# A hybrid RWKV-7 / latent-attention layer: TensorE's order in the recurrence stage written out by hand

## The chip, the cores and the metric

The kernel runs on one core of a Trainium2 chip. The metric is the device time of one execution in microseconds. Before the change three runs took 2447.49, 2455.89 and 2457.13 us, median 2455.89 us.

## What is computed

One layer over 2048 tokens of width 1024, in float32. One input projection feeds an RWKV-7 branch (8 heads of 64), a latent-attention branch (8 heads) and two sigmoid gates; the gated sum of the branches goes through an output projection, a norm and a residual add. Cut to what the change touches:

```
u    = rmsnorm(h, g_pre)
proj = u @ w_in                       # 1024 x 5152
feat_a, z_a, c_q, c_kv, k_pe, z_b, gate_logits = split_cols(proj, ...)

# RWKV-7 branch, per head, over the tokens t in order
f = feat + mu * (prev(feat) - feat);  r, k, v, wd, ad = split_cols(f, ...)
w = exp(-DECAY_SCALE * sigmoid(w0 + tanh(wd) @ w_decay_up));  a = sigmoid(a0 + ad @ w_iclr_up)
kk = k * k_k / max(norm(k * k_k), 1e-12);  k = k * (1 + (a - 1) * k_a)
sa = S @ -kk_t
S  = S * w_t + sa (kk_t * a_t)^T + v_t k_t^T
y_t = S @ r_t
y = groupnorm(y) + sum(r * k * r_k) * v
y_a = (y * silu(z_a)) @ w_out_a
# latent attention on c_q, c_kv, k_pe gives y_b (not touched)
merged = sigmoid(g_a) * y_a + sigmoid(g_b) * y_b
h = h + rmsnorm(merged @ w_o, g_post)
```

## The kernel before

**Stages.** The sequence is four segments of 512 tokens (NS) for the projection and eight half-steps of 256 tokens (NH) for the recurrence, each of four chunks of 64 tokens. The program writes: the projection of segment 0 (`proj_seg(0)`), the element work of half-step 0 (`elem(0)`), then in turn recurrence steps and projections of segments 1 to 3, then steps 5 to 7, preparations for attention, step 8 and the gate columns (`gates_seg`). Attention and the output stage follow. From about 185 us to 1142 us the recurrence's small products run with projection matmuls between them.

**The projection.** `proj` (L287) and `mm3` (L279) compute one tile of 128 columns by 512 tokens, `pj`, in 24 matmuls: for each of eight row blocks three (L283 to L285), since weight and input are each split into a high and a low part (`whl`; `xh`, `xl`). `make_xT` (L207) normalises x and transposes it (`xps`). Weights come over SP's DMA queue (`load_w`, L253). A tile's result is shifted by a token and written to memory (`fsh`), or copied (`lat`). `gates_seg` (L487) does the same for 42 gate tiles; when a segment's X isn't the one in place, it reloads it (`load_xT`).

**The recurrence.** `step(k)` (L833) works on half-step k and finishes half-step k-1:

- `zblock` (L637) multiplies the half-step's vectors into the blocks `pz`, masked to `Zr` by DVE (L646), one per chunk; pieces go to memory (`d_q`).
- `gather` (L653) reads them back as `Xg`, and `invert` (L691) inverts small triangular blocks by 60 DVE operations in pairs (L698, L700), writes the result to `d_q` and reads it as `Xinv`. `merge` (L716) joins the blocks: DVE's `XT` (L721), PE's `pf` and `px` (L726, L735), copies into `Zr` (L743).
- `chunk` (L745) of half-step k-1 is a chain between engines: `ch` from `Zr` (L756), ACT's `rs`, `ch` from `Xinv` (L772), ACT's `uv`, `ch` from `BT` (L778), DVE's new `uv` (L782), which the next chunk needs. The `Y` products (L296, L301, L785) collect its output y.
- `gnorm` (L794) normalises y, transposes it (`ypt`, L814) and adds the bonus, which it reads from and writes to memory (`bvb`, `d_ya`, L818 to L820). `tokmaj` (L663) transposes `bs` and `vf` (`pb`, `pv`).
- `elem` (L509) prepares half-step k+1: norms (`n`, `Rn`), three `bc` tiles (L551, evacuated at L553), then for each of four head pairs the logits `wa` (L585), the normalisation `rn` (L604) and DVE, ACT and POOL work (`cum` L592, `kkn`, `AR`, `BK`, `bv`). `bc`, `wa`, `rn` and `bo` share one PSUM buffer.

**Order.** Engines work in order, each on its own list. Before the change a list scheduler with a simulated timeline orders all engines: it takes an instruction when its inputs are ready by its own costs, and by place in the program among those that are ready. A step runs `elem`, `invert`, `gnorm` and `tokmaj` as generators and takes them in turn by a string, in the program's order only:

```python
for ch in "itietiegtietietii":
    next({"i": inv, "t": tm, "g": gn, "e": el}[ch], None)
```

Of the kernel before, what the change touches and what calls it, by code (L numbers as in the profile page):

```python
# [49 lines left out]
def hybrid_layer(ctx, tc, x, positions, g_pre, w_in, b_gate, mu_shift, w0, w_decay_up, a0, w_iclr_up, k_k, k_a,  # L50
# [156 lines left out]
    def make_xT(pool, psp, ptag, pbufs, s, g_rep, Xs):  # L207

        XH, XL = Xs
        for i in range(4):  # L210
# [18 lines left out]
            for k in range(2):  # L229
# [63 lines left out]

    def pin(*args, **kw):

        tc.keep_in_program_order(PE.matmul(*args, **kw))  # L296
# [7 lines left out]
    with st:  # L304
# [19 lines left out]
        NZ = 6  # L324
# [106 lines left out]
        def proj_seg(s):  # L431
            make_xT(sa, ppa, "pj", 2, s, g_rep, X)
# [10 lines left out]
            proj(ps, wtile(1536, elo=G if s else V, keep=later(0)), X, 2)  # L443
# [3 lines left out]
            yield  # L447
            for p in range(NP):
                ps = pj()
                proj(ps, wtile(512 + p * P, keep=later(p)), X)  # L450
                f = shift(ps, 4 + p)
                nc.sync.dma_start(d_f["k", p, s], f)
                yield
            for i, c0 in enumerate((C_CQ, C_CQ + P, C_CKV)):
                ps = pj()
                proj(ps, wtile(c0, keep=later(i)), X)
# [3 lines left out]
                yield  # L460

            for p in range(NP):
                for nm, c0, j in (("r", 0, 0), ("v", 1024, 8)):
                    ps = pj()
                    proj(ps, wtile(c0 + p * P, keep=later(j // 8)), X)
                    f = shift(ps, j + p)
                    nc.sync.dma_start(d_f[nm, p, s], f)
                    yield
# [3 lines left out]
            proj(ps[0:HD, :], load_w(sa, None, KC, HD, pieces=[(0, 32, k1), (32, 16, k1[:, 16:32]),  # L472
# [12 lines left out]
            yield  # L485

        def gates_seg():  # L487

            xs = NS - 1
            for s, i in d_zg:  # L490
                if s != xs:
                    xs = s
                    load_xT(X, s)
                ps = pj()
                c0 = (C_ZA, C_ZB, C_G, C_G + 4 * P, C_G + 8 * P, C_G + 12 * P)[i // 4] + (i % 4) * P
                proj(ps, wtile(c0), X)
# [7 lines left out]
                yield  # L504
# [4 lines left out]
        def elem(hs, E):  # L509
# [11 lines left out]
            for p in range(NP):  # L521
# [6 lines left out]
                          skip_group_check=True)  # L528
            lats = []
            for i in range(3):  # L530
# [7 lines left out]
                          skip_group_check=True)  # L538
            nr = t_("sqe", 2)
# [8 lines left out]
            for i in range(3):  # L548
# [7 lines left out]
                G.dma_start((d_cq[s][:, i, :, :] if i < 2 else d_kv[s])[:, :, cs_], lhl)  # L556
            hl = [se.tile([P, 256], F32R, name=f"hl{k}", tag=f"hl{k}", bufs=1) for k in range(2)]
# [19 lines left out]
            for p in range(NP):  # L577
# [24 lines left out]
                G.tensor_scalar(ta, ta, 0.5, 0.5, op0=ALU.mult, op1=ALU.add)  # L602
                rn = pp.tile([P, 2, 256], F32, name="rn", tag="e", bufs=1)
# [23 lines left out]
                if p == NP - 1:  # L627
                    bo = pp.tile([P, 2, 256], F32, name="bo", tag="e", bufs=1)
                    bonus(bo[:, 1], *last)()
# [61 lines left out]
        def invert(hs, E):  # L691
# [3 lines left out]
            for s_ in range(1, 31):  # L695
# [5 lines left out]
                if s_ % 5 == 0:  # L701
                    yield
# [11 lines left out]
            yield  # L714

        def merge(hs, E):  # L716
# [12 lines left out]
            for h in range(2):  # L729
                A.copy(FT[h * HD + 32:h * HD + 64], pf[h * HD + 32:h * HD + 64])  # L730
# [702 lines left out]
```

## Time and profile before

| | before |
|---|---|
| median of three runs | 2455.89 us |
| the profiled execution, and its span | 2453.57 us, 2451.8 us |
| PE busy in the span | 2211.4 us (90%) |
| DVE, ACT, POOL busy | 1089.6 (44%), 712.1 (29%), 1017.4 us (41%) |
| mean granted clock of PE | 0.950 |
| chain that ended last | PE 57%, DVE 16%, DMA 14% |
| merges (`pf`) of steps 0 to 7 begin at | 270, 405, 509, 619, 742, 864, 979, 1075 us |

The span is the time from the first to the last instruction. PE is TensorE, DVE VectorE, ACT ScalarE, POOL GpSimd, SP the engine that issues most DMAs. A busy PE is one with a matmul in it, at whatever clock; the granted clock is a share of 2.4 GHz, so 1.00 is that and 0.50 is 1.2 GHz, and values between are means over a stretch. Idle time before an instruction is put down to the instruction or DMA that ended it.

### The profile page before, as it was taken

The numbers are of one execution on the slowest core, as the hardware profiler recorded it, in microseconds if no ns is written. First come the engines' busy times: TensorE is split into PE (matmuls) and PEld (weight loads), VectorE is DVE, ScalarE is ACT, GpSimd is POOL, SyncE is SP. The second block draws the span as 40 slices with busy tenths as digits, with TensorE's granted clock in tenths as the row PEclk, the third lists the DMA queues.
The fourth block names the chain that finished last, engine by engine and source line by source line (L and its number), as shares of the span: only waits on it lengthen the run. The fifth ranks groups of instructions, "written<-read, shape, count | busy, mean of one in ns | idle before, by whom it ended". The sixth has DMA issues, their size and how long they took to land.

```text
span 2451.8 us, 37859 instructions
## 1 busy us (share of the span) xinstructions
PE 2211.4 (90%) x14313; PEld 1644.0 (67%) x14313; DVE 1089.6 (44%) x2007; ACT 712.1 (29%) x1283; POOL 1017.4 (41%) x1194
## 2 busy tenths in 40 slices
PE   6968989988979898997799998988999989999997
PEld 5747767767757676775555655555678867788876
DVE  7166575678374847434453534345130231300312
ACT  4343242343224343122233333332331211111111
POOL 6474352455254645222345653554533232312422
PEclk9969999989989999999798999999999999999999
DMA  7768867647658788673221112050396885766873
GB/s 249 229 190 276 258 194 232 172 125 220 187 169 247 208 254 262 181 216 104 65 82 31 50 58 76 28 190 7 106 367 224 290 309 197 287 203 202 317 243 120
DMA packets 315182, 455.15 MB, mean 186 GB/s; under 512 B 114044, under 2 KB 207288, under 8 KB 309368
## 3 DMA queue, kind: packets, MB, share of 16 engines
q1 hardware_dynamic: 285112, 406.06, 51.8%
q0 software_dynamic: 12608, 42.47, 5.3%
q10 hardware_dynamic: 17280, 4.20, 1.1%
q8 instruction: 113, 1.85, 0.3%
q14 instruction: 69, 0.57, 0.1%
HBM read 313.69 MB, written 132.64 MB: 182 GB/s over the span
## 4 chain that ended last, share of the span: by engine, by line
PE 57%; DVE 16%; DMA 14%; POOL 5%; issue 3%; ACT 2%; SPq 1%; ACTq 0%; DVEq 0%; POOLq 0%
PE pj L283 7%; PE pst L296 7%; PE pj L284 7%; PE pj L285 7%; PE po L296 5%; DVE mx L1055 3%; DMA wraw<-in_w_in_dram 2%; DMA whl<-d_wi 2%; PE pout L283 2%; PE pout L284 2%; PE pout L285 2%; PE py L283 2%; PE py L284 2%; PE py L285 2%; DVE Xg L700 2%
## 5 line engine op out<-in xcount | busy, mean ns | idle before, releaser
L283 PE MATMUL pj<-xh,whl 128*128 128x512 f32 (+1 forms) x1320 | 531.3, 403 | 31.3 <-DMA whl<-d_wi 13.9
L285 PE MATMUL pj<-xh,whl 128*128 128x512 f32 (+1 forms) x1320 | 526.4, 399 | 2.4 <-POOL whl L248 2.4
L284 PE MATMUL pj<-xl,whl 128*128 128x512 f32 (+1 forms) x1320 | 525.5, 398 | 0.0
L1178 POOL TENSOR_TENSOR acc<-acc,pt 128x1024 f32<-128x1024 f32 (+2 forms) x144 | 290.6, 2018 | 206.9 <-PE po L296 179.6
L283 PEld LDWEIGHTS pj<-xh,whl 128*128 128x128 f32 x1320 | 252.9, 192 | 97.8 <-issue 12.1
L285 PEld LDWEIGHTS pj<-xh,whl 128*128 128x128 f32 x1320 | 252.5, 191 | 63.0 <-POOL whl L248 4.2
L284 PEld LDWEIGHTS pj<-xl,whl 128*128 128x128 f32 x1320 | 253.0, 192 | 55.9 <-issue 2.5
L1055 DVE TENSOR_REDUCE mx<-pm 128x2 f32<-128x1024 f32 (+3 forms) x160 | 164.5, 1060 | 150.4 <-PE pm L296 149.7
L248 POOL TENSOR_TENSOR whl<-wraw,whl 128x512 fp32r<-128x512 f32 (+1 forms) x114 | 145.9, 1281 | 161.6 <-ACT whl L247 149.6
L1358 DVE SCALAR_TENSOR_TENSOR tg<-tg,py 128x512 f32<-128x512 f32 x64 | 43.9, 687 | 307.5 <-PE py L285 204.9
L1165 ACT ACTIVATE pt<-pst 128x1024 f32<-128x1024 f32 (+2 forms) x144 | 125.6, 885 | 165.0 <-PE pst L296 150.5
L1360 POOL TENSOR_TENSOR tg<-tg 128x512 f32<-128x512 f32 x32 | 41.3, 1290 | 214.1 <-DVE tg L1358 214.1
L247 ACT CAST whl<-wraw 128x512 fp32r<-128x512 f32 (+1 forms) x116 | 71.5, 616 | 184.0 <-DMA wraw<-in_w_in_dram 98.5
L296 PE MATMUL po<-pt,Vt 128*64 128x512 f32 (+3 forms) x576 | 121.7, 539 | 0.0
L283 PE MATMUL py<-BH,whl 128*128 128x512 f32 x256 | 103.9, 407 | 12.5 <-DVE tg L1358 11.8
L296 PE MATMUL pm<-KH,QH 64*128 64x512 f32 (+3 forms) x312 | 71.8, 446 | 39.4 <-DVE mx L1055 35.0
L284 PE MATMUL py<-BL,whl 128*128 128x512 f32 x256 | 103.0, 403 | 0.0
L285 PE MATMUL py<-BH,whl 128*128 128x512 f32 x256 | 102.9, 402 | 0.0
L284 PE MATMUL pout<-wf,MH 128*128 128x512 f32 x256 | 101.0, 395 | 0.0
L285 PE MATMUL pout<-wf,ML 128*128 128x512 f32 x256 | 99.5, 395 | 0.0
L283 PE MATMUL pout<-wf,MH 128*128 128x512 f32 x256 | 97.1, 394 | 0.0
L698 DVE TENSOR_TENSOR tq<-Xg,Qg 128x30 f32<-128x30 f32 (+7 forms) x240 | 80.6, 336 | 33.1 <-DMA Xg<-d_q 27.8
(372 smaller groups left out, 3971.0 us busy)
## 6 DMA issues: line engine op xcount, KB each, us to landing
whl<-d_wi SPq DMA_DIRECT2D x222, 512.0 KB
d_wi<-whl SPq DMA_DIRECT2D x80, 512.0 KB
wraw<-in_w_in_dram SPq DMA_DIRECT2D x98, 256.0 KB
whl<-d_wo SPq DMA_DIRECT2D x48, 512.0 KB
wf<-d_wf SPq DMA_DIRECT2D x48, 512.0 KB
cqt<-d_cq POOLq DMA_DIRECT2D x16, 1024.0 KB, 5.4
d_zg<-thg SPq DMA_DIRECT2D x42, 256.0 KB
xl<-d_x POOLq DMA_DIRECT2D x8, 1024.0 KB, 11.0
```

The costliest lines, as they stand in the source:

```text
L247: (ehi.copy if ehi is A else ehi.tensor_copy)(hi, src)
L248: elo.tensor_tensor(lo, src, f32(hi), op=ALU.subtract)
L283: mm(ps, lhsT=lh, rhs=rh, start=(i == 0), stop=False)
L284: mm(ps, lhsT=lh, rhs=rl, start=False, stop=False)
L285: mm(ps, lhsT=ll, rhs=rh, start=False, stop=(stop and i == n - 1))
L296: tc.keep_in_program_order(PE.matmul(*args, **kw))
L698: V.tensor_tensor(t3, Xg[:, 0:m, s_:s_ + 1].to_broadcast([P, m, n]), Qg[:, s_:s_ + 1, s_ + 1:32].to_broadcast([P, m, n]), op=ALU.mult)
L700: V.tensor_tensor(Xg[:, 0:m, s_ + 1:32], Xg[:, 0:m, s_ + 1:32], t3, op=ALU.add)
L1055: V.tensor_reduce(mx[:, :, j, c], pm[:, :, 0:w], axis=AX.X, op=ALU.max)
L1165: A.activation(pt[:, :, q0:512], pst[:, :, q0:512], AF.Exp, scale=scale)
L1178: G.tensor_tensor(acc[:, :, q0:512], acc[:, :, q0:512], pt[:, :, q0:512], op=ALU.add)
L1358: V.scalar_tensor_tensor(tg, tg, 1.0, po, op0=ALU.add, op1=ALU.mult)
```

## The change

From the end of `elem(0)` to the end of step 8 and the gates, PE is taken from the scheduler: it gets the instructions in the order in which the program writes them (`tc.manual_schedule`). The other engines are scheduled as before. So the program now writes the order: `proj_units` gives the projection out in units of three matmuls, `step` yields a weight at each place between pieces, and `weave` puts as many units into a place as the weight's share of the step's 80 (58 in step 8) is of the segment's 151 units, or of the gates' 350. `make_xT` counts two units for four transposes; the reload of X in `gates_seg` counts 14, for which places stay empty.

The step's pieces are in a new order: two chunks with z blocks 0 and 1, gnorm of chunks 0 and 1, z blocks 2 and 3, `gather`, the whole inversion at one place and with a higher priority (400) on the scheduled engines, then chunks 2 and 3 with parts of `elem`. `gnorm` is split into the normalisation of y, which follows its chunks, and `outputs`. No matmul is added or left out.

```diff
+    def proj_units(ps, w, X, cut=1):
+        XH, XL = X
+        for i in range(cut):
+            t = slice(i * 512 // cut, (i + 1) * 512 // cut)
+            for c in range(KC):
+                (lh, ll), rh, rl = w[c], XH[:, c, t], XL[:, c, t]
+                PE.matmul(ps[:, t], lhsT=lh, rhs=rh, start=(c == 0), stop=False)
+                PE.matmul(ps[:, t], lhsT=lh, rhs=rl, start=False, stop=False)
+                PE.matmul(ps[:, t], lhsT=ll, rhs=rh, start=False, stop=(c == KC - 1))
+                if (i * KC + c) % cut == cut - 1 and (i, c) != (cut - 1, KC - 1):
+                    yield 1
...
@@ gates_seg
                     load_xT(X, s)
+                    yield 14
...
@@ invert
                 V.tensor_tensor(Xg[:, 0:m, s_ + 1:32], Xg[:, 0:m, s_ + 1:32], t3, op=ALU.add)
-                if s_ % 5 == 0:
-                    yield
...
@@ step
+            for c in range(2):
+                it = ch(c)
+                next(it)
+                z(c)
+                yield 1
+                next(it)
+                yield 2
+                for _ in it:
+                    pass
+                yield 2
+            if Ep:
+                gnorm(Ep, 0)
+            z(2)
+            yield 1
+            z(3)
             if E:
-                zblock(k, E, 0)
-                zblock(k, E, 1)
-            if Ep:
-                chunk(k - 1, Ep, 0, Ep["uv"][1])
...
+                gather(k, E)
+                with tc.high_priority(offset=AHEAD):
+                    invert(k, E)
+            yield 1
+            for c in range(2, 4):
+                it = ch(c)
+                for w in (1, 2):
+                    next(it)
+                    next(el, None)
+                    yield w
+                for _ in it:
+                    pass
+                next(el, None)
+                yield 2
             if Ep:
+                gnorm(Ep, 1)
+            next(el, None)
+            yield 2
...
-            for ch in "itietiegtietietii":
-                next({"i": inv, "t": tm, "g": gn, "e": el}[ch], None)
-                yield
...
+            for ch_ in "ttetetetegetegeee":
+                next({"t": tm, "g": gn, "e": el}[ch_], None)
+                yield 2
...
+                yield 8
+                for _ in merge(k, E):
+                    yield 4
+                yield 3
...
+        def weave(ks, fill, units):
+            total = sum(WS if k < NH else WL for k in ks)
+            have = 0.0
+            for k in ks:
+                for w in step(k):
+                    have += w * units / total
+                    while have >= 1:
+                        have -= next(fill, 1)
...
+        order_.enter_context(tc.manual_schedule(engines={mybir.EngineType.PE}))
+        WS, WL, UN, UG = 80, 58, 16 * 8 + 7 + 16, 42 * 8 + 14
         for s in range(1, NS):
-            for k in (0,) if s == 1 else (2 * s - 3, 2 * s - 2):
-                run(step(k))
-            run(proj_seg(s))
-        for k in range(2 * NS - 3, NH):
-            run(step(k))
+            filler = proj_seg(s)
+            weave((0,) if s == 1 else (2 * s - 3, 2 * s - 2), filler, UN)
...
+        filler = gates_seg()
+        UL = WL * UG // (3 * WS + WL)
+        weave(range(2 * NS - 3, NH), filler, UG - UL)
```

Three places show how instructions move. Lines of the changed kernel are some 20 higher (L302 to L304 are its projection).

PE, last chunk of step 4, around the Xinv product. Before:

```order
L285 MATMUL pj<-xh,whl 128x512
L772 MATMUL ch<-rs,Xinv_433 64x64 x8
L604 MATMUL rn<-Rn,selr 128x256
L567 MATMUL rn<-rf,blk_120 128x256
L283 MATMUL pj<-xh,whl 64x512
L284 MATMUL pj<-xl,whl 64x512
```

After:

```order
L542 MATMUL n_6822<-sqe,s_hd 32x256
L302 MATMUL pj<-xh,whl 128x512
L303 MATMUL pj<-xl,whl 128x512
L304 MATMUL pj<-xh,whl 128x512
L792 MATMUL ch<-rs,Xinv_433 64x64 x8
L553 MATMUL n_6822<-sqe,s_cq 32x256
L302 MATMUL pj<-xh,whl 128x512
```

Before, 18 projection matmuls stand ahead of the Xinv product and 21 between the `rn` behind it and the `BT` product (a run's first or last rows are shown). After, three stand ahead of it, a norm's product `n` behind it, and then six. Over the whole stretch the projection is in 271 runs where it was in 195. Between a step's first and last z block stand 36 to 42 projection matmuls in steps 1 to 4, and behind the last one some 174.

DVE, step 3, the evacuations of the three `bc` tiles (`cum<-cum,prm,bc`, `Pi<-...`, `u<-...`) and the inversion (`tq`, `Xg`). Before:

```order
L546 SCALAR_TENSOR_TENSOR Rn<-nh,losgn,sqe 128x256
L782 TENSOR_TENSOR uv<-ch,sp 64x256 x2
L236 TENSOR_TENSOR xl<-xps,xh 128x4x128
L553 SCALAR_TENSOR_TENSOR cum<-cum,prm,bc 128x256
L236 TENSOR_TENSOR xl<-xps,xh 128x4x128
L553 SCALAR_TENSOR_TENSOR Pi<-Pi,prm,bc 128x256
L809 TENSOR_REDUCE v_5835<-y_5833 128x8
L698 TENSOR_TENSOR tq<-Xg,Qg 128x30
L700 TENSOR_TENSOR Xg<-Xg,tq 128x30
L553 SCALAR_TENSOR_TENSOR u<-u,prm,bc 128x256
```

After:

```order
L719 TENSOR_TENSOR tq<-Xg,Qg 128x56
L721 TENSOR_TENSOR Xg<-Xg,tq 128x14x4
L719 TENSOR_TENSOR tq<-Xg,Qg 128x42
L721 TENSOR_TENSOR Xg<-Xg,tq 128x14x3
L719 TENSOR_TENSOR tq<-Xg,Qg 128x30
L571 SCALAR_TENSOR_TENSOR cum<-cum,prm,bc 128x256
L721 TENSOR_TENSOR Xg<-Xg,tq 128x15x2
L719 TENSOR_TENSOR tq<-Xg,Qg 128x15
L721 TENSOR_TENSOR Xg<-Xg,tq 128x15
L571 SCALAR_TENSOR_TENSOR Pi<-Pi,prm,bc 128x256
```

Before, two of the three stand ahead of the inversion's first operation and the third behind its first pair. After, the first stands behind 29 of its 30 pairs and the others behind all. In steps 2, 4 and 5 the first stands behind 24 pairs, in the others of 1 to 6 behind 25 to 29.

DVE, step 3, `XT` (which needs the inverse back from memory) and the element work of the next half-step (`cum` scan, `AR`, `kkn`, `BK`). Before:

```order
L561 TENSOR_TENSOR hl_6507<-wat,hl_6507 64x256
L607 SCALAR_TENSOR_TENSOR kkn<-kf,prm,rn 128x256
L571 TENSOR_TENSOR bv<-rn,vf 128x256
L615 SCALAR_TENSOR_TENSOR AR<-kkn,Pt 128x4x64
L561 TENSOR_TENSOR hl_6508<-wat,hl_6508 64x256
L617 TENSOR_TENSOR kkn<-kkn,ta 128x256
L621 TENSOR_TENSOR BK<-kkn,Pi 64x4x64
L721 STREAM_TRANSPOSE XT<-Xinv_433 32x512
L571 TENSOR_TENSOR bv<-bo,vf 128x256
L721 STREAM_TRANSPOSE XT<-Xinv_433 32x512
```

After:

```order
L571 SCALAR_TENSOR_TENSOR u<-u,prm,bc 128x256
L739 STREAM_TRANSPOSE XT<-Xinv_433 32x512 x2
L709 COPY uv<-pv 64x256 x2
L611 SCALAR_TENSOR_TENSOR cum<-scanm,th 128x256
L636 TENSOR_TENSOR AR<-rf,Pt 128x4x64
L346 SCALAR_TENSOR_TENSOR fsh<-pj,dv,mf 128x511
L347 SCALAR_TENSOR_TENSOR fsh<-pj,dv,halo 128x1
L627 SCALAR_TENSOR_TENSOR kkn<-kf,prm,rn 128x256
```

Before, `XT` stands at the end of the element work. After, it stands ahead of the first `cum` scan, and all four parts of the element work behind it. So it is in steps 1 to 4; in steps 5 and 6 one `cum` scan stands ahead of a part of `XT`.

## Rows read from the trace of the kernel before

**Rows 1.** Busy time and clock of the stretch that the change touches.

```profile
core 0: us, PE busy (x) PEld busy (x) DVE busy (x) ACT busy (x) POOL busy (x), PEclk, DMA share, GB/s
...
185.00:1142.00 957.00, 872.70 (x7075) 672.78 (x7073) 579.74 (x1296) 324.46 (x672) 406.16 (x589) 0.95 0.70 207
```

**Rows 2.** The same columns for the two halves of step 4.

```profile
619.00:680.00 61.00, 61.00 (x600) 45.79 (x600) 25.89 (x63) 20.56 (x41) 15.40 (x26) 1.00 0.64 185
680.00:742.00 62.00, 49.32 (x272) 36.90 (x270) 46.63 (x95) 18.12 (x38) 35.70 (x45) 0.86 0.59 176
```

**Rows 3.** The same halves, the projection's matmuls and their readers alone (without POOL).

```profile
619.00:680.00 61.00, 38.25 (x150) 27.02 (x150) 4.48 (x11) 4.14 (x6) 1.00 0.64 185
680.00:742.00 62.00, 42.13 (x156) 29.35 (x154) 5.91 (x11) 3.17 (x5) 0.86 0.59 176
```

**Rows 4.** PE's waits from 185 to 1142 us: total us, times, longest us.

```profile
PE ypt L814 <- DVE y L812: 12.4, 5, 8.3
PE wa L585 <- DVE bv L571: 10.1, 8, 2.4
PE pj L283 <- DMA whl<-d_wi: 7.6, 4, 3.0
PE Y L301 <- DVE bvb L818: 6.8, 2, 4.0
...
PE wa L585 <- DVE kkn L607: 5.5, 2, 4.0
PE rn L604 <- ACT ta L589: 4.8, 6, 1.4
PE Y L296 <- DVE bvb L818: 4.2, 1, 4.2
PE pj L283 <- ACT lat L458: 3.8, 1, 3.8
```

**Rows 5.** The chain of waits in step 2: start us, us.

```profile
445.10 0.43 DVE uv L782
445.56 0.70 DVE Zr L646
...
450.51 8.67 DMA Xg<-d_q
...
496.42 4.10 DMA d_q<-Xg
500.57 3.31 DMA Xinv<-d_q
```

**Rows 6.** DVE's groups from 185 to 1142 us: the inversion.

```profile
L700 DVE TENSOR_TENSOR Xg<-Xg,tq 128x30 f32<-128x30 f32 (+7 forms) x240 | 86.3, 359 | 5.1
L698 DVE TENSOR_TENSOR tq<-Xg,Qg 128x30 f32<-128x30 f32 (+7 forms) x240 | 80.6, 336 | 33.1 <-DMA Xg<-d_q 27.8
```

**Rows 7.** The chain of waits in step 6, a projection matmul at the lower clock.

```profile
939.75 0.43 PE pj L284
```

**Rows 8.** PE's timeline in the element work of half-step 0: start us, us.

```profile
142.87 0.58 PE L604 MATMUL rn<-Rn,selr 128*128 128x256 f32 x1 [6.76 <-ACT ta L589]
...
168.62 0.58 PE L604 MATMUL rn<-Rn,selr 128*128 128x256 f32 x1 [2.83 <-ACT ta L589]
```

**Rows 9.** The columns of rows 1 for most of that stage.

```profile
140.00:175.00 35.00, 16.66 (x66) 11.59 (x66) 28.57 (x44) 15.72 (x31) 30.99 (x45) 0.51 0.54 157
```

**Rows 10.** PE's timeline at full clock around a small product.

```profile
1044.39 0.40 PE L285 MATMUL pj<-xh,whl 128*128 128x512 f32 x1
1044.62 0.39 PE L283 MATMUL pj<-xh,whl 128*128 128x512 f32 x1
1044.94 0.68 PE L772 MATMUL ch<-rs,Xinv 64*64 64x64 f32 x16
1045.56 0.50 PE L284 MATMUL pj<-xl,whl 128*128 128x512 f32 x1
```

**Rows 11.** PE's waits from 1142 to 1200 us.

```profile
PE pn L296 <- DVE QL L248: 19.6, 1, 19.6
```

More of the change, by code (lines that the diff above doesn't have):

```diff
@@ L431, in proj_seg @@
         def proj_seg(s):
-            make_xT(sa, ppa, "pj", 2, s, g_rep, X)
+            yield from make_xT(sa, ppa, "pj", 2, s, g_rep, X)
             if s == 0:
@@ L442, in proj_seg @@
             ps = pj()
-            proj(ps, wtile(1536, elo=G if s else V, keep=later(0)), X, 2)
+            yield from proj_units(ps, wtile(1536, elo=G if s else V, keep=later(0)), X, 2)
             f = shift(ps, 12)
@@ L446, in proj_seg @@
             nc.sync.dma_start(d_wa[s], f)
-            yield
+            yield 1
             for p in range(NP):
                 ps = pj()
-                proj(ps, wtile(512 + p * P, keep=later(p)), X)
+                yield from proj_units(ps, wtile(512 + p * P, keep=later(p)), X)
                 f = shift(ps, 4 + p)
                 nc.sync.dma_start(d_f["k", p, s], f)
-                yield
+                yield 1
             for i, c0 in enumerate((C_CQ, C_CQ + P, C_CKV)):
                 ps = pj()
-                proj(ps, wtile(c0, keep=later(i)), X)
+                yield from proj_units(ps, wtile(c0, keep=later(i)), X)
                 f = sa.tile([P, 512], F32, name="lat", tag="fsh", bufs=2)
@@ L464, in proj_seg @@
                     ps = pj()
-                    proj(ps, wtile(c0 + p * P, keep=later(j // 8)), X)
+                    yield from proj_units(ps, wtile(c0 + p * P, keep=later(j // 8)), X)
                     f = shift(ps, j + p)
                     nc.sync.dma_start(d_f[nm, p, s], f)
-                    yield
+                    yield 1
             ps = pj()
             k1 = w_in[:, C_KPE:C_KPE + 32]
-            proj(ps[0:HD, :], load_w(sa, None, KC, HD, pieces=[(0, 32, k1), (32, 16, k1[:, 16:32]),
+            yield from proj_units(ps[0:HD, :], load_w(sa, None, KC, HD, pieces=[(0, 32, k1), (32, 16, k1[:, 16:32]),
                                                                (48, 16, k1[:, 0:16])], key="kpe"), X)
@@ L538, in elem @@
                           skip_group_check=True)
+                if i < 2:
+                    yield
             nr = t_("sqe", 2)
@@ L838, in step @@
             el = elem(k + 1, new_E(k + 1)) if k + 1 < NH else iter(())
-            if E:
-                zblock(k, E, 0)
-                zblock(k, E, 1)
-            if Ep:
-                chunk(k - 1, Ep, 0, Ep["uv"][1])
-            if E:
-                zblock(k, E, 2)
-            yield
-            if Ep:
-                chunk(k - 1, Ep, 1, Ep["uv"][2])
-            if E:
-                zblock(k, E, 3)
-                gather(k, E)
-            next(el, None)
-            yield
-            if Ep:
-                chunk(k - 1, Ep, 2, Ep["uv"][3])
-                chunk(k - 1, Ep, 3, uvq[0])
@@ L857, in step, with ch @@
[L857 to L869 removed]
+            def ch(c):
+                return chunk(k - 1, Ep, c, Ep["uv"][c + 1] if c < 3 else uvq[0]) if Ep else iter((None, None))
@@ L871, in run @@
+            for ch_ in "ttetetetegetegeee":
+                next({"t": tm, "g": gn, "e": el}[ch_], None)
+                yield 2
+            for g in (tm, gn, el):
+                for _ in g:
+                    yield 2
+            if E:
+                yield 8
+                for _ in merge(k, E):
+                    yield 4
+                yield 3
         def run(g_):
             for i, _ in enumerate(g_):
-                if ropes and i == 4:
+                if ropes and i == 42:
@@ L939, in hybrid_layer @@
         attn_weights(0, sw, 2, tmp[:, 2], (sb, "XT"))
-        run(step(NH))
+        weave((NH,), filler, UL)
         def value(t):
@@ L947, in value @@
             V.tensor_copy(Vt[1][:, t, :], ps[:, 3 * P:512])
-        run(gates_seg())
+        for _ in filler:
+            pass
+        order_.close()
         pst.close()
```

76 lines of the change are left out of this document (42 added, 34 removed).

## The prediction

> **What bounds the kernel now.** I read the busy times by stretch first. The change touches the stretch from 185 us (recurrence with projections of segments 1 to 3 and the gates) to 1142 us: PE is busy for 872.70 of 957 us there, at a mean granted clock of 0.95, DVE for 579.74, POOL for 406.16 [rows 1]. So PE bounds it, and there are two things to win: 957 - 872.70 = 84.3 us of idle PE, and what the low clock costs. At full clock one projection matmul follows another after 0.23 us (1044.39 to 1044.62) [rows 10], at the lower level (1.2 of 2.4 GHz) after 0.43 us [rows 7]. A clock of 0.95 means 2 x 0.05 x 957 = 96 us at the lower level; while PE is busy (0.91 of the time) it loses 0.20 of 0.43 there, so some 41 us in all.
>
> Where that idle time lies is told by the two halves of one step. From 619 to 680 us, where the chunks and the z blocks are, PE is busy for 61.00 of 61.00 us at clock 1.00; from 680 to 742 us, where the inversion and the element work of the next half-step are, for 49.32 of 62 us at clock 0.86, and DVE for 46.63 [rows 2]. Both halves hold about as many projection matmuls, 150 and 156 [rows 3]. The first half has more cover than it can use, the second too little. By the list of PE's waits the idle time is `ypt` for the normalised y 12.4 us, `pj` for weights and evacuation 7.6 + 3.8, `Y` for the bonus that comes back by DMA 6.8 + 4.2, and the element pieces `wa` and `rn` for DVE and ACT 10.1 + 5.5 + 4.8 [rows 4].
>
> **The change, term by term.** No matmul is added or dropped; the sum is made against the profiled execution, 2453.57 us (2.3 us below the median 2455.89).
>
> *Waits that go: -34.8 us.* By the new order only 36 to 42 projection matmuls stand between a step's first and last z block, and 174 of a step's some 216 behind it (steps 1 to 4). y of chunk 1 is normalised right after that chunk, some 100 projection matmuls (100 x 0.23 = 23 us) ahead of its `ypt`, so 12.4 us go. The weights are used at an even pace of three matmuls per unit: 7.6 + 3.8 go. Between the second `ypt` and the next `Y` stand 45 to 81 projection matmuls, 10 to 19 us, for the write and read that cost 6.8 + 4.2 [rows 4]: 11.0 go. 12.4 + 11.4 + 11.0 = 34.8. What could keep a part: no DMA is added, but the bonus's DMAs share SP's queue with the projection's weight loads, which are now issued at other times.
>
> *A new wait at `bc`: +30 us.* The inversion's 60 operations now stand ahead on DVE; the evacuations of the three `bc` tiles stand behind 48 to 58 of them in steps 1 to 6 (second place of the order shown), where they stood ahead of nearly all. `bc` has one PSUM buffer, so the second `bc` on PE waits for the first one's evacuation. Its time after the last z block: the evacuation of the z block to the arrival of Xg is 445.56 to 450.51 + 8.67 = 459.18, 13.6 us [rows 5]; 24 pairs at 359 + 336 ns are 16.7 us [rows 6] (up to 29 pairs in steps 1 and 3, where PE has more cover); 15 other DVE operations stand between, at the stretch's mean of 579.74 / 1296 = 0.45 us [rows 1] 6.7 us; in sum 37 us. PE's cover up to the second `bc`: 60 to 66 projection matmuls in steps 1 to 4, 75 in steps 5 and 6, so 14 to 17 us, and two chunks, transposes and small tiles, some 180 records at 22.75 us for 600 - 150 = 450 of them [rows 2, 3], 9 us more: 23 to 27 us. PE comes there later by the waits that it has had in between, some 2 us. That leaves about 10 us as the upper end per step; the lower end is 0, since in the present order the same evacuations wait for nothing but PE. No row shows this order; I take the middle, 5 us, in each of steps 1 to 6, since 13.6 us of gather and the mean of a pair are from stretches in which DVE and the queues had other work between. Next is XT: behind the inversion's end it needs d_q written and read, 4.10 + 3.31 us [rows 5], and now stands ahead of the first `cum` of the element work on DVE (third place of the order shown). PE reaches `wa` about then, so I cost that at nothing; uncovered it is 7.4 us a step.
>
> *The element pieces closer together: -4 us.* From the first `wa` to the fourth PE has 18 us of cover in steps 1 to 4 and 21 us in steps 5 and 6, by 51 to 63 projection matmuls and the small pieces. What DVE needs for one of the four parts is bounded by the stage where nothing covers it: the `rn` of 142.87 and of 168.62 us are three parts apart, 8.6 us each [rows 8]. From 140 to 175 us, four parts, DVE is busy for 28.57 us [rows 9], 7.1 us a part. At 7.1 the three parts need 21 us: PE waits 3 us in each of four steps and, with the tail of the last part, 2 us in two: 16 us, in place of the 10.1 + 5.5 + 4.8 = 20.4 us of `wa` and `rn` now. Bounds: 0, and at 8.6 us a part 7.6 x 4 + 5 x 2 = 40 us.
>
> *Chunks with little cover: +14 us.* Three projection matmuls (0.7 us) before the Xinv product, six before the others, where 12 to 24 stood. The evacuations they wait for are two of 0.43 us after the handing over [rows 5]: about 1.1 us in all. Say 0.4 us in each of 24 chunks, and the full 1.1 us in the four chunks of step 7, where the reload of X takes 14 units out of the filling: 9.6 + 4.4 = 14. Bounds 0 and 28 x 1.1 = 31.
>
> *More changes between kinds of matmul: +8 us.* The projection is cut into 271 runs instead of 195. Going to a small product costs 0.32 - 0.23 = 0.09 us, coming back about 0.11 [rows 10]: 76 x 0.2 = 15, and half of the new boundaries are at transposes; I take 8.
>
> *Clock: -14 us.* PE's work of the second halves becomes denser (174 where 156 stood, and less idle time), so I take a third of the 41 us back. Bounds: all of it, and a loss of as much.
>
> *Change to attention: -10 us.* Past 1142 us PE waits 19.6 us for QL behind a chain of loads on SP [rows 11], and these stand behind the last bonus writes on SP's queue. In the new order the last `ypt` has 63 dense projection matmuls (63 x 0.23 = 14.5 us) behind it, where the last chunk's work stood before, so the loads can start earlier; the small key and value products lose their places between the last chunks. I take half of the 19.6; bounds 0 and all.
>
> Sum: -34.8 + 30 - 4.4 + 14 + 8 - 14 - 10 = -11.2, so **2442 us**, 0.6% below the median. A measurement of this kernel can tell about 0.5%, 12 us, from no change; the forecast is close to that line.
>
> **The rivals.** (a) *The new waits don't arise*: the bc evacuations are in time and the element work keeps up. For it: all of DVE's work is 579.74 of 957 us [rows 1], and z blocks with 36 to 42 projection matmuls between them start the gather earlier in a step than now, when chunks with 12 to 24 matmuls at each place stood between. Then 30 and 16 us drop out: 2442 - 46 = 2396 us.
> (b) *DVE becomes the bound in every step*: inversion, XT and the element work stand in one row on DVE, where they were mixed. From the last z block: 37 us to the bc evacuations, the rest of the inversion 4, d_q 7.4, four parts at 7.1 to 8.6 make 28 to 34, so 76 to 82 us. PE's work from there to the step's end is 174 x 0.23 = 40 us of projection and, if the other products take what they take in the first half, 61.00 - 38.25 = 22.75 us [rows 2, 3], some 63 us. It decides as soon as a part takes over 6 us of DVE between two `rn` and XT really blocks `cum`. Price: `bc` at its upper end, 12 x 4 + 10 x 2 = 68 in place of 30, and parts at 8.6 us, 40 in place of 16: 2442 + 38 + 24 = 2504 us. Against it: the parts' DVE work can run ahead of PE.
> (c) *The clock falls more often*: short runs of projection with short waits between them. In the half with waits the clock was 0.86, in the one without it 1.00 [rows 2]; if the new order spreads waits over both halves, the first halves fall too, and the loss of 41 us grows to 75 instead of shrinking by 14: 2442 + 48 = 2490 us. The Trainium skill, TensorE: Matmul & The Clock Gate, section "A second HAM failure mode: psum-queue depth-cycling", speaks for this one: a PE that idles for a moment between groups of matmuls often enough has its clock go down and up again, and pays between the bursts. The trace agrees only as far as its halves differ in clock; no row shows runs of six matmuls under this order.
> (d) *The waits only change their names*: what is won at `ypt` and `Y` is lost at `bc` and `cum`, and the change to attention starts no sooner: 2442 + 10 = 2452 us.
>
> **How the numbers follow.** Chances: forecast 0.45 (its own range 2415 to 2465), (a) 0.20, (b) 0.18, (c) 0.09, (d) 0.08. Faster by over 0.5% (below 2443.6): 0.20 of (a) and somewhat over half of the forecast's own, 0.29: 0.49. Slower by over 0.5% (above 2468): (b) 0.18, (c) 0.08, 0.01 of the forecast's: 0.27. Within: the other 0.24. The range 2380 to 2498 leaves out a quarter of (a) and rather more than half of (b), under 0.2.
>
> **What would show it.** Right: in the second halves PE's waits at `ypt` (for y) and at `Y` (for bvb) are gone; `bc` or the `wa` behind it waits for DVE's evacuations, 3 to 7 us a step; DVE's first `cum` of a part is preceded by XT waiting for Xinv; the wait for QL is about 10 us; the clock of the stretch is 0.96 to 0.97 or more. Wrong: `bc` without any wait (then (a)), `wa` and `rn` waiting over 40 us in sum (then (b)), a clock below 0.93 (then (c)). If the projection's wait for whl grew beyond 15 us, weight loads would be late, which I have costed at nothing.

## The result, and the profile after

The changed kernel took 2561.44 us (median of 4 runs, 2551.27 to 2563.27) beside 2453.73 us of the kernel before: a ratio of 1.043, 95% interval 1.040 to 1.047. It is slower by 107.7 us, where 2442 us was forecast. The profiled execution has a span of 2558.0 us, 106.2 more than before; PE is busy for 2215.1 us of it (2211.4 before), DVE for 1107.0.

The stretch now ends at about 1225 us instead of 1142. First the windows view of the changed kernel, with the columns of [rows 1]:

```profile
185.00:1225.00 1040.00, 854.04 (x7004) 650.37 (x7004) 589.57 (x1278) 325.01 (x665) 398.05 (x590) 0.91 0.65 190
```

The stretch is idle for 1040 - 854.04 = 186 us, where it was 84.3 [rows 1]. Its clock is 0.91 instead of 0.95. The two stretches do not hold quite the same work: 104 small products of attention and some 32 projection matmuls that stood ahead of 1142 us now come behind 1225. Up to the first `pn` of attention, which begins at 1175.58 us before and at 1284.36 after, the same 7725 matmuls have run. Before, then after:

```profile
185.00:1175.58 990.58, 881.12 (x7107) 678.69 (x7106) 590.51 (x1312) 326.34 (x676) 412.09 (x611) 0.94 0.70 206
```

```profile
185.00:1284.36 1099.36, 890.55 (x7168) 677.15 (x7168) 612.07 (x1319) 338.34 (x690) 405.03 (x615) 0.90 0.64 187
```

PE is idle for 208.8 us instead of 109.5 and busy for 9 us more (61 small products more lie behind 185 us). So of the 109 us by which `pn` is later, 99 are idle PE; behind it nothing is lost. PE's waits in the stretch up to 1225 us (total us, times, longest):

```profile
PE pb L692 <- POOL bs L689: 61.9, 11, 9.4
PE rn L624 <- ACT ta L608: 27.7, 17, 3.9
PE xps L232 <- DVE xt L228: 20.4, 4, 7.4
PE ch L799 <- ACT uv L794: 15.7, 11, 2.8
PE bo L586 <- DVE rf L645: 14.5, 7, 3.8
PE wa L604 <- DVE bv L590: 13.0, 6, 4.0
PE pj L302 <- DMA whl<-d_wi: 12.1, 4, 3.8
...
PE ch L775 <- DVE uv L803: 5.4, 3, 3.3
PE ch L792 <- ACT rs L778: 2.8, 1, 2.8
PE wa L604 <- DVE kkn L627: 2.0, 2, 1.2
PE rn L586 <- DVE rf L645: 1.6, 3, 0.9
...
PE bc L569 <- DVE Pi L571: 0.4, 1, 0.4
```

Against [rows 4], `ypt` waiting for y and `Y` waiting for bvb are gone, as forecast. `bc`, which was to wait for 30 us, waits for 0.4. In its place `pb` waits for POOL's `bs` 61.9 us, some 7 to 9 us once in each of steps 1 to 7, and 0.4 to 1.5 us at a later `pb` in four of them. `rn`, `wa` and `bo` wait 27.7 + 13.0 + 2.0 + 14.5 + 1.6 = 58.8 us, `xps` 20.4, the chunk's `ch` 15.7 + 5.4 + 2.8.

One of the waits of `pb`, step 4, from the timelines of the four engines (start us, us; in brackets idle time before and what ended it):

```profile
724.25 0.19 DVE L719 TENSOR_TENSOR tq<-Xg,Qg 128x30 f32<-128x30 f32 x1 [2.69 <-DMA Xg<-d_q]
...
732.79 0.39 PE L304 MATMUL pj<-xh,whl 128*128 128x512 f32 x1
...
734.23 1.28 ACT L559 ACT_TABLE_LOAD   x1 [4.16 <-DVE sqe L558]
...
735.97 1.75 DVE L560 RECIPROCAL sqe<-sqe 128x256 f32<-128x256 f32 x1 [0.82 <-ACT sqe L559]
...
738.55 0.67 DVE L826 TENSOR_REDUCE v<-y 128x8 f32<-128x512 f32 x1
...
739.60 1.12 POOL L689 TENSOR_TENSOR bs<-BK,pcs 128x512 f32<-128x512 f32 x1
...
740.77 1.12 PE L692 MATMUL pb<-ident,bs 128*128 128x128 f32 x4 [7.59 <-POOL bs L689]
```

PE's last projection matmul ahead of `pb` starts at 732.79; `pb` starts at 740.77. `bs` takes the buffer that y2, the squared y of chunks 2 and 3, has held, so POOL may start it (739.60) when DVE has summed y2 (738.55, `v`); on POOL's list it also stands directly behind an operation on that sum. The sum stands behind 13 pairs of the inversion and half of a 14th, and behind a reciprocal that waits for ACT's root, which loads a function table first (734.23, 1.28 us). The inversion itself starts late, after 2.69 us of waiting for Xg. The chain of waits goes on through the same step (start us, us):

```profile
716.86 7.27 DMA Xg<-d_q
...
755.47 6.07 DMA d_q<-Xg
...
762.49 2.42 DMA Xinv<-d_q
...
764.94 0.71 DVE XT L739
765.67 0.69 DVE cum L611
```

Xg needs 7.27 us, the inversion lasts until 755, writing and reading the inverse take 6.07 + 2.42 us more, `XT` ends at 765.6, and only then comes the first `cum` of the element work. The merge of that step starts at 796 us: from the inversion's first operation 796 - 724 = 72 us.

Past 1225 us, PE's wait for QL in the changed kernel:

```profile
PE pn L310 <- DVE QL L249: 15.2, 1, 15.2
```

It was 19.6 us [rows 11]; 4.4 us are gained there, not 10.

### The profile page after: what moved, and what is told of

Its sections match the earlier page's. It is cut to its first block, busy times and chain, and to the rows that moved or that the text cites. A ratio compares the mean times of both kernels' runs of the same rounds, so it can differ in the third digit from the quotient of the medians.

```text
span 2558.0 us, 37877 instructions
## 1 busy us (share of the span) xinstructions
PE 2215.1 (87%) x14313; PEld 1638.8 (64%) x14313; DVE 1107.0 (43%) x2007; ACT 716.4 (28%) x1283; POOL 1008.1 (39%) x1194
## 4 chain that ended last, share of the span: by engine, by line
PE 51%; DVE 20%; DMA 15%; POOL 5%; issue 4%; ACT 3%; SPq 2%; ACTq 0%; DVEq 0%; POOLq 0%
PE pst L310 7%; PE po L310 5%; PE pj L302 3%; PE pj L284 3%; PE pj L285 3%; DVE tq L719 3%; PE pj L286 3%; DVE mx L1127 3%; DVE Xg L721 3%; PE pj L303 3%; PE pj L304 3%; DMA whl<-d_wi 3%; DMA wraw<-in_w_in_dram 2%; PE pout L284 2%; PE pout L285 2%
## 5 line engine op out<-in xcount | busy, mean ns | idle before, releaser
L302 PE MATMUL pj<-xh,whl 128*128 128x512 f32 (+2 forms) x912 | 394.3, 432 | 19.0 <-DMA whl<-d_wi 12.1
L304 PE MATMUL pj<-xh,whl 128*128 128x512 f32 (+2 forms) x912 | 367.1, 403 | 2.6 <-POOL whl L249 2.5
L303 PE MATMUL pj<-xl,whl 128*128 128x512 f32 (+2 forms) x912 | 367.3, 403 | 0.0
L302 PEld LDWEIGHTS pj<-xh,whl 128*128 128x128 f32 (+1 forms) x912 | 180.4, 198 | 78.9 <-issue 23.5
L304 PEld LDWEIGHTS pj<-xh,whl 128*128 128x128 f32 (+1 forms) x912 | 179.7, 197 | 48.1 <-POOL whl L249 4.4
L303 PEld LDWEIGHTS pj<-xl,whl 128*128 128x128 f32 (+1 forms) x912 | 180.6, 198 | 30.7
L284 PE MATMUL pj<-xh,whl 128*128 128x512 f32 x408 | 160.6, 394 | 9.0 <-DMA whl<-d_wi 5.5
L285 PE MATMUL pj<-xl,whl 128*128 128x512 f32 x408 | 159.9, 392 | 0.0
L286 PE MATMUL pj<-xh,whl 128*128 128x512 f32 x408 | 159.6, 391 | 0.0
L719 DVE TENSOR_TENSOR tq<-Xg,Qg 128x30 f32<-128x30 f32 (+7 forms) x240 | 87.3, 364 | 41.8 <-DMA Xg<-d_q 35.0
```

Of the source, the lines that this page charges most:

```text
L284: mm(ps, lhsT=lh, rhs=rh, start=(i == 0), stop=False)
L285: mm(ps, lhsT=lh, rhs=rl, start=False, stop=False)
L286: mm(ps, lhsT=ll, rhs=rh, start=False, stop=(stop and i == n - 1))
L302: PE.matmul(ps[:, t], lhsT=lh, rhs=rh, start=(c == 0), stop=False)
L303: PE.matmul(ps[:, t], lhsT=lh, rhs=rl, start=False, stop=False)
L304: PE.matmul(ps[:, t], lhsT=ll, rhs=rh, start=False, stop=(c == KC - 1))
```

## The experiments

Each run is one core; times are medians beside the kernel before in the same runs (2451 to 2459 us).

**The hand order alone undone** (`e1_list_pe`; three rounds as `e11_list_pe_again`):

```diff
-        order_.enter_context(tc.manual_schedule(engines={mybir.EngineType.PE}))
```

> The changed program, but PE is ordered by the list scheduler again; only the hand order is undone, the new order of the pieces (z blocks early, gnorm split, units of three) stays. If the hand order is at fault (PE has to wait at a place where the scheduler would have taken something else, and DVE's order follows from it): 2440 to 2480 us, the wait of pb for bs under 15 us. If the new order of the pieces is at fault (z blocks early, so that the inversion stands ahead of other work on DVE whoever orders PE): 2530 to 2570 us. If short runs of projection and the clock are at fault: the runs get longer again, clock 0.95, 2450 to 2480 us.

> The kernel of e1_list_pe once more, in three rounds, since it is below the kernel before: 2425 to 2440 us, an interval of the ratio wholly below 0.995.

Measured: 2429.43 us, ratio 0.989 [0.984, 0.994]; again 2427.91 us, 0.989 [0.987, 0.991]. So the hand order costs 2561.44 - 2427.91 = 133.5 us, and the rest of the change is worth 27 us over the kernel before: it beats both. Which of its parts brings that was not taken apart. The windows line up to the first `pn`, and the wait of `pb`, of the first of the two runs:

```profile
185.00:1155.98 970.98, 877.45 (x7128) 674.76 (x7127) 585.29 (x1313) 328.92 (x678) 410.62 (x611) 0.94 0.70 210
```

```profile
PE pb L692 <- POOL bs L689: 6.2, 5, 2.6
```

PE is idle for 970.98 - 877.45 = 93.5 us, 16 less than before, at a clock of 0.94. `pb` waits only 6.2 us for `bs`, though the two share a buffer there too and though in steps 2 to 7 the sum of y2 stands behind 21 to 30 pairs of the inversion, even more than in the change: PE has other work in its list meanwhile. The theory that the new order of the pieces is at fault whoever orders PE fell; the old order of the pieces, written out by hand, was not run.

**Another buffer for y2** (`e2_y2_own`; the edit puts it into that of `XT`, which is free at that time):

```diff
-            y2 = sb.tile([P, 8, HD], F32, name="y2", tag="bs", bufs=1)
+            y2 = sb.tile([P, 8, HD], F32, name="y2", tag="XT", bufs=1)
```

> The changed kernel with one edit: y2, the squared y of gnorm, gets a buffer that is free at that time (that of XT) instead of sharing that of bs. Theory of the shared buffer: bs on POOL, and so pb on PE, waits until DVE has summed y2, which stands behind 14 to 18 pairs of the inversion; with its own buffer the wait of pb (61.9 us in 11) falls under 15 us. If all of it is gained: 2495 to 2515 us. If it moves to bc, whose evacuation also stands behind the inversion: bc or wa wait 20 to 40 us more, 2525 to 2550 us. If the clock and the short runs cost the time: 2550 us or more.

Measured: 2511.1 us, ratio 1.022 [1.019, 1.025], 50 us faster than the change. Its waits:

```profile
PE rn L624 <- ACT ta L608: 26.0, 13, 6.1
...
PE bc L569 <- DVE Rn L564: 18.7, 6, 3.6
...
PE pb L692 <- POOL bs L689: 5.0, 5, 2.8
```

`pb` fell from 61.9 to 5.0 us; 18.7 us of it come back at `bc`, whose `Rn` stands behind the inversion too. With PE in the list scheduler's hands the same edit gains nothing:

> PE by the list scheduler (as in e1_list_pe) and y2 in its own buffer. In e1_list_pe pb waited 6.2 us for bs, in the kernel before about as long, so there is little to gain: 2420 to 2435 us, the same as e1_list_pe. If the shared buffer also held DVE's order back there: 2390 to 2415 us.

Measured: 2445.57 us, ratio 0.997 [0.996, 0.998], outside both ranges: 16 to 18 us slower than without it (`e1_list_pe`, `e11_list_pe_again`). Why it loses there is not shown. So the shared buffer costs something only in the hand order, and with y2 apart in both the hand order costs 2511.1 - 2445.57 = 66 us.

**The norms of the next half-step earlier** (`e3_norms_early`), and both edits (`e4_both`):

```diff
             for c in range(2):
                 next(it); z(c)
+                next(el, None)
                 yield 1
                 next(it)
+                next(el, None)
                 yield 2
...
                 gnorm(Ep, 1)
-            next(el, None)
```

> The changed kernel with one edit: the norms of the next half-step (four squares, two of the latents) are taken in chunks 0 and 1 instead of 2 and 3, bc in chunks 2 and 3, wa and rn from the start of the next part. So DVE's reciprocal and bc stand at 0 to 13 pairs of the inversion instead of 13 to 29, and one or two of the four cum scans stand in the inversion. y2 and bs still share a buffer. Theory of DVE's order: rn, wa and bo wait half as long as the 57 us now, pb still waits (its v sum is only 3 to 5 pairs earlier, some 45 us in sum): 2500 to 2535 us. If short runs and clock are the cause: 2550 us or more.

> Both edits: y2 in a buffer of its own and the norms early. Theory of DVE's order: pb's wait under 15 us, rn, wa and bo under 40 us, clock back to 0.94 or more: 2450 to 2490 us. If the clock and the short runs are the cause: 2540 us or more. If it stays between, at 2490 to 2540, PE's cover in the first part of a step is what lacks.

Measured: 2560.57 us (1.042 [1.038, 1.046]) and 2529.23 us (1.029 [1.025, 1.034]): nothing is gained alone, and with y2 apart it loses 18 us. Both expectations from DVE's order fell. In `e4_both` `pb` still waits for `bs` 25.1 us, without the shared buffer: POOL, too, works its list in order, and other operations stand ahead of `bs`. Waits of the first:

```profile
PE bc L569 <- DVE Xg L721: 29.0, 6, 6.5
...
PE rn L624 <- ACT ta L608: 4.5, 4, 1.8
```

`rn` waits for `ta` 4.5 us instead of 27.7, but `bc` now waits 29.0 us, where the profile names `Xg`: the `Rn` that it reads stands among the inversion's first pairs on DVE (713.24 us in step 4, behind the first pair and half of the second), and these wait for the gather (2.82 us).

**The inversion queued behind the norms on DVE**, in the change (`e6_inv_behind_norm`) and in the best hand order (`e10_more_inv_late`):

```diff
-                with tc.high_priority(offset=AHEAD):
-                    invert(k, E)
...
                 gnorm(Ep, 1)
             next(el, None)
+            with tc.issue_after(Es[k + 1]["Rn"]):
+                invert(k, E)
```

> The changed kernel with one edit: on DVE the inversion is queued behind the norms of the next half-step (behind Rn), so the reciprocal, Rn and the sums of gnorm(1) stand ahead of it; y2 and bs share their buffer as in the change. Theory: the inversion stood too early in DVE's order, ahead of work that PE waits for, because the schedule took Xg to arrive sooner than it does. Then pb's wait of 61.9 us falls under 20 us although the buffer is shared, bc is in time: 2500 to 2530 us. Theory of the shared buffer alone: pb still waits 40 us or more, and XT comes later: 2550 us or more. If all DVE work simply fills the step whatever its order, pb's wait goes and as much appears at rn, wa and pf: 2540 to 2565 us.

> e8_more_at_elem with one edit: on DVE the inversion is queued behind Rn of the next half-step, so the norms and the sums of gnorm(1) stand ahead of it. Theory of DVE's order (what PE waits for stands behind the inversion): bc, rn and wa lose 25 us of their 48: 2455 to 2470 us. Theory that DVE's whole row sets the step, whatever its order: XT and the last parts come later by as much, 2480 to 2500 us.

Measured: 2547.25 us (1.038 [1.036, 1.040]), 14 us better than the change; and 2488.21 us (1.013 [1.011, 1.016]), no better than `e8_more_at_elem` at 2484.97. Waits of the two:

```profile
PE pb L692 <- POOL bs L689: 38.5, 10, 6.0
```

```profile
PE wa L604 <- DVE bv L590: 22.2, 6, 5.1
PE bo L586 <- DVE rf L645: 19.9, 6, 5.0
...
PE pj L302 <- DMA whl<-d_wi: 11.9, 5, 5.0
...
PE wa L604 <- DVE kkn L627: 8.0, 5, 2.0
```

In the first `pb` still waits 38.5 us, though the sum of y2 stands ahead of the inversion in steps 1 to 6: the place behind the inversion is only a part of that wait. In the second `bc` and `pb` are no longer there, but `wa`, `bo` and the weight loads take more than that back. Moving the inversion to and fro on DVE changes where PE waits and hardly how long. The priority of 400 does nothing at all: in the program without it every engine's instructions stand in the same order.

**The place of the projection.** In runs of twelve (`e7_runs_of_12`, on `e2_y2_own`):

```diff
                     have += w * units / total
-                    while have >= 1:
-                        have -= next(fill, 1)
+                    if have >= 4:
+                        while have >= 1:
+                            have -= next(fill, 1)
```

> e2_y2_own with one edit: places hand out no unit until four are due, then all of them, so that projection comes in runs of 12 or more, with places in between that have none. Theory of thin cover: where a run stands the waits vanish, elsewhere they grow; the sum of PE's waits stays within 20 us: 2490 to 2535 us. Theory of the clock and of the changes between kinds of matmul: long runs keep the clock, 0.95 and 2440 to 2480 us.

Measured: 2558.27 us, 1.043 [1.040, 1.045], 47 us slower than `e2_y2_own` and outside both ranges, at a mean clock of 0.928 (0.937 there). Longer runs (a median of 15 projection matmuls instead of 6) don't bring the clock back; the places left without projection wait longer, and PE is idle for 214.9 us up to `pn` instead of 163.3. The theory of the clock and of the changes between kinds of matmul fell as it was put. What long runs would do without the added idle time is not shown.

More of it at transposes and element work, less around the merge (`e8_more_at_elem`, on `e2_y2_own`):

```diff
                 next({"t": tm, "g": gn, "e": el}[ch_], None)
-                yield 2
+                yield 3
...
-                yield 8
+                yield 2
                 for _ in merge(k, E):
-                    yield 4
-                yield 3
+                    yield 1
+                yield 1
...
-        WS, WL, UN, UG = 80, 58, 16 * 8 + 7 + 16, 42 * 8 + 14
+        WS, WL, UN, UG = 86, 75, 16 * 8 + 7 + 16, 42 * 8 + 14
```

> e2_y2_own with one edit: more of a step's projection stands at the places of the transposes and the element work (weight 3 instead of 2 at each), less at its end before and in merge (4 instead of 15). Theory of thin cover at the element work: rn, bc, bo and wa wait half as long (36 us less of 72), nothing new at the end: 2465 to 2490 us. Theory that DVE's row of work sets the step's length: what is won there is lost at the end of the step (pf, or z for Zr and BK): 2500 to 2520 us.

Measured: 2484.97 us, 1.013 [1.011, 1.015], 26 us faster than `e2_y2_own`, the best hand order. Its stretch and waits:

```profile
185.00:1149.00 964.00, 835.55 (x7002) 634.30 (x6999) 568.05 (x1279) 323.79 (x664) 401.04 (x590) 0.95 0.69 204
```

```profile
PE wa L604 <- DVE bv L590: 21.5, 9, 3.1
PE xps L232 <- DVE xt L228: 18.1, 3, 7.4
PE ch L799 <- ACT uv L794: 16.0, 9, 3.2
PE bo L586 <- DVE rf L645: 13.0, 6, 3.0
PE rn L624 <- ACT ta L608: 12.6, 10, 2.3
PE bc L569 <- DVE Rn L564: 11.1, 5, 3.4
```

The two edits together take 76 us off the change: idle PE from 186 to 964 - 835.55 = 128 us, 57 us, and 854.04 - 835.55 = 18 us of busy time for the same matmuls (7004 and 7002 records), at a clock of 0.95 instead of 0.91. Against the kernel before, up to `pn`, the change is busy for only 9 us more. So by these rows the low clock had a price of at most some 18 us in the change; no run takes it alone.

Transposes of x further apart (`e9_xt_spaced`, on `e8_more_at_elem`: `yield 5` for four transposes instead of 2), and the weight moved to the four element parts (`e12_fill_at_parts`, on `e2_y2_own`: 1 at transposes, `bc` and norms, 4 at `wa`, `rn`, `bo`):

> e8_more_at_elem with one edit: the four transposes of a group count five units instead of two, so a segment's 32 transposes stand 2.5 times as far apart (and their places hold less projection). Theory: PE waits 18 us at them since DVE's xt comes later than a dense row of transposes asks for; spaced, 5 us or less are left: 2468 to 2478 us. If the cover taken from these places is missed there (chunk's uv, rs): 2485 to 2500 us.

> e2_y2_own with one edit: the weights at the transposes, bc and the norms fall to 1 and those at the four parts of the element work (wa, rn, bo) rise to 4, the places in merge fall from 15 in sum to 4. Between wa and rn, and between rn and the next wa, then stand 18 to 24 projection matmuls, as many as in the list-scheduled e1_list_pe (medians 20 and 23) where e8_more_at_elem has 15 and 9. Theory of the cover's place: wa, rn and bo wait under 20 us in sum (50 in e8_more_at_elem), bc and pb 10 us more: 2450 to 2470 us. Theory that DVE's row of work from the last z block on sets a step's length, wherever the projection stands: 2480 to 2505 us, with the waits at bc and pb.

Measured: 2528.03 us (1.030 [1.028, 1.032]), 43 us slower than `e8_more_at_elem`; and 2519.59 us (1.027 [1.023, 1.031]), 35 slower, and 8 slower than `e2_y2_own`. Both are outside both ranges I gave. Waits of each:

```profile
PE xps L232 <- DVE xt L228: 22.4, 3, 10.0
...
PE pb L692 <- POOL bs L689: 17.9, 8, 5.9
...
PE pz L315 <- DVE Zr L667: 15.4, 6, 7.1
```

```profile
PE bc L569 <- DVE Rn L564: 17.2, 6, 4.1
PE pb L692 <- POOL bs L689: 15.8, 10, 4.7
PE wa L604 <- DVE bv L590: 14.1, 6, 3.9
...
PE pj L302 <- DMA whl<-d_wi: 10.4, 4, 3.3
...
PE rn L624 <- ACT ta L608: 2.7, 1, 2.7
```

In the first, `xps` waits as long as before (22.4 us), and `pz` and `pb` wait for what these steps' places lack. Spacing could not help, because PE waits at the first transpose of a segment and hardly at the others: 5.5, 7.3 and 7.4 us in the change, 4.5, 10.0 and 8.0 here. Its lines for segment 3 in the change:

```profile
575.42 1.06 ACT L220 ACTIVATE xjunk<-xt 128x1024 bf16<-128x1024 f32 x1 [3.09 <-DMA d_kr<-kr]
```

```profile
578.89 1.12 PE L232 MATMUL xps<-ident,xt 128*128 128x128 f32 x4 [7.35 <-DVE xt L228]
```

ACT squares x into `xjunk`, which shares its buffers with `kr`, the last result of the segment before, and waits until that has been written to memory; then POOL and DVE make `xt`. It is so in segments 2 and 3; in segment 1 ACT waits for the load of x (1.31 us). No run parts these two buffers.

In the second `rn`, `wa` and `bo` do fall, to 2.7 + 14.1 + 2.3 + 1.8 = 21 us from 50, near the expectation, but `bc`, `pb` and the weight loads (`pj` for `whl`, 23.7 us on DMA, POOL and ACT) take more than that back. Between an `rn` and the next `wa` the edit brought the median only to 12 matmuls, not to the 18 to 24 that were expected.

More projection in steps 5 to 7, less behind the last merge, in the change (`e13_gates_early`) and in the best hand order (`e14_gates_early_best`):

```diff
-        UL = WL * UG // (3 * WS + WL)
+        UL = 10
```

> The changed kernel with one edit: of the gates' 350 units 340 instead of 282 are spread over steps 5 to 7 and 10 are left for step 8 (in the changed kernel 260 projection matmuls stand behind the last merge, in the kernel before 71, in e1_list_pe 25). Theory: these 190 matmuls (44 us) are cover that steps 5 to 7, idle for 20 + 23 + 18 us, lack, while the last stretch with its dense matmuls idles for 1 us and does not need it: 2520 to 2535 us. Theory that DVE's row sets the steps' length: steps 5 to 7 keep their length, the last stretch gets shorter by 44 us, about the same 2515 to 2530. If cover at these places doesn't help because PE waits at a few places only: the steps get longer by the added work, the last stretch shorter: 2550 to 2565 us.

> e8_more_at_elem with the same edit. Steps 5 to 7 idle there for 14 + 16 + 12 us, the last stretch for 3. Theory: 25 to 40 us are gained, 2445 to 2460 us, level with the kernel before. If PE waits at a few places only: 2475 to 2490 us.

Measured: 2555.32 us (1.042 [1.039, 1.044]) and 2494.07 us (1.015 [1.012, 1.018]): 6 us faster than the change, within the spread of its runs, and 9 slower than `e8_more_at_elem`, outside both ranges. By the merges, steps 5 to 7 idle for 14 + 28 + 11 us (20 + 23 + 18 in the change), the last stretch for 9 instead of 1: 162 matmuls more in front of the last merge take 8 us of idle time off there, and 8 come up behind it. More cover at the same places does not remove these waits.

## Why the prediction was wrong

- **What bounds the kernel** was right: PE's idle time between 185 us and attention. Up to `pn` it grew by 99 us instead of shrinking.
- **Waits that go (-34.8 us):** right for `ypt` and `Y`, 12.4 + 11.0 us, and for `lat`; wrong for `whl`, which went from 7.6 to 12.1 us.
- **A new wait at `bc` (+30 us): the step that failed first.** I saw that the work on DVE behind the inversion would be late and worked out 10 us a step as the upper end, but followed only one of the things that stand there. `pb` comes ahead of `bc` on PE, needs `bs`, and `bs` needs the buffer of y2, whose sum stands behind the inversion too. PE waited there first, 61.9 us, and so came late enough to `bc` (0.4 us). `e2_y2_own` shows that it is the buffer: with y2 apart 50 us are gone. The inversion ahead of the sum is the smaller part: with it out of the way (`e6_inv_behind_norm`) `pb` keeps 38.5 us and 14 us are gained.
- **The element pieces (-4 us):** mis-sized. `wa` and `rn` wait 27.7 + 13.0 + 2.0 = 42.7 us for the releasers that cost 20.4 before, where 16 was forecast and 40 was my upper bound; `rn` for `rf`, and `bo`, add 16.1, where they took 2.8. The 7.1 us a part were about right (`cum` at 765.67 us, two parts on at 778.77: 6.6 us each), but behind `XT` PE had less cover than the mean I used: 9 projection matmuls is the median between an `rn` and the next `wa`, 23 in the list-scheduled order. That `XT` ahead of `cum` costs nothing was an assumption without a row. I also overlooked a second shared buffer: `ta`, for which `rn` waits, has one for all parts, so ACT may write the next only when DVE's `kkn` (L637) of the part before has read the last. From the tile view of `ta`, the time that ACT sat idle for it from 185 to 1225 us (4.0 in the kernel before):

```profile
  DVE kkn L637: 17.0, 12
```

Some 16 of the 27.7 us of `rn` come behind these waits. No run gives `ta` a second buffer.

- **Not in the sum at all:** `xps` for `xt`, 20.4 us (0.8 + 2.3 in all for `xps` before). All but 0.2 us of it is at the first transpose of a segment, which has a fixed place and, in segments 2 and 3, comes behind the buffer of `kr`. What would help is open.
- **Chunks (+14 us):** 23.9 us at `ch` (3.3 before), inside the bounds of 0 to 31.
- **More changes between kinds of matmul (+8 us):** no run takes them alone. With 138 runs of projection instead of 258 up to 1250 us (`e7_runs_of_12`) PE is busy for 885.2 us up to `pn` beside 886.1 in `e2_y2_own`, at a lower clock.
- **Clock (-14 us):** the wrong sign. It fell to 0.91, with a price of at most some 18 us, beside 99 us of idle time; so rival (c) is not what decided. The Trainium skill, TensorE: Matmul & The Clock Gate, "A second HAM failure mode: psum-queue depth-cycling", tells of such changes of the clock in another kernel, whose PE idles for moments between groups of matmuls. The clock did fall here too, but making the runs longer (`e7_runs_of_12`) made it no better.
- **Change to attention (-10 us):** mis-sized. The wait for QL is 4.4 us shorter; of the idle time from 1142 to 1175.58 us before and from 1225 to 1284.36 us after, 25.2 and 22.9 us, 2.3 are gone.
- **Rival (b)**, DVE as the bound of every step, came nearest: 2504 us from `bc` at its upper end (68) and parts at 40. Measured are 61.9 at `pb` and 58.8 at the parts; `xps`, the chunks and the clock make the rest. Its row of work came out too: from the last z block to the last `BK` pass 78 to 81 us in steps 1 to 4 (89 and 90 in steps 5 and 6), where it had 76 to 82, and to the merge 82 to 88 us, of which PE is busy for 64 to 67, where it had 63. Step 4 from its last z block to its merge:

```profile
713.96:796.29 82.33, 65.52 (x407) 47.96 (x403) 59.51 (x142) 26.61 (x56) 36.12 (x62) 0.92 0.61 171
```

But DVE is busy for only 59.5 of these 82.3 us: the row is a chain with waits in it, not a full engine. It is shorter with y2 apart (76 to 77 us to the merge in steps 1 to 4 of `e2_y2_own`), and queueing the inversion elsewhere (`e6`, `e10`) doesn't cure it.

- **The signs I gave** pointed three ways: `bc` without a wait was to mean (a), and it came with the opposite result; `wa` and `rn` over 40 us meant (b), a clock below 0.93 (c). The first rested on `bc` being the only place to wait.
- Of some 133 us that the hand order costs, 50 are the buffer and 26 the places of the projection; with them undone 57 us remain. The waits of `e8_more_at_elem` are many and short, mostly 1 to 3 us each but for `xps`, at places whose cover is fixed. That the list scheduler escapes them because it puts many matmuls in one place and none in another (0 to 78 between an `rn` and the next `wa` in `e1_list_pe`) fits, but no run shows it: neither more cover (`e13`) nor cover moved (`e9`, `e12`) brought it. This stays open.

## What to carry to other kernels

An order written by hand fixes where an engine waits: every place needs cover for the latest thing behind it, and a uniform share of filler is not that. Before taking one engine from the scheduler, list for each place what releases it, through buffers that are shared as well as through data, and look where that releaser stands on its own in-order engine. Here three of the large waits led to a shared buffer: `bs` and y2, which a run shows, and `ta` and `kr`, which the traces show and no run took away. A rearrangement and a change of who orders should be measured apart: here the first was worth 27 us and the second cost 133.

## What the runs showed that I had not expected

ACT's root in the norms loads a function table first, 1.28 us (734.23 us), on the path of DVE's reciprocal and all that stands behind it; another of 1.28 us (762.13 us) stands directly ahead of the `th` and `ta` for which the first `rn` of that step waits 2.82 us. And adding projection to steps that idle for 61 us (`e13_gates_early`) took only 8 us of that away: 162 matmuls at 0.23 us are 37 us of cover, and most of it came to places that were not waiting. The three steps grew by 4 + 8 + 12 us.
